# A GEGLU MLP on one core: the 4x2x4 algorithm in the down phase from pass 3 instead of 4, with the preparation of w_down moved to earlier passes

## The chip, the cores and the metric

One core of a Trainium2 chip. The time is device time of one execution in microseconds (us). Most executions of one kernel agree within 0.3%.

Engines by the names of the profile: PE is TensorE (matmul), PEld its weight loads, DVE is VectorE, ACT is ScalarE, POOL is GpSimd, SP is SyncE, which here only issues DMAs. "L827" is line 827 of the kernel's file. Lines shift a little from kernel to kernel, because each edit adds some: the fast gate/up matmuls are L827 before and L843 after, the older gate/up matmuls L620 and L621, the older down phase L966 and L983, the fast one L1074 and L1091.

## The reference

```python
# x: 8 x 1024 x 1024, w_gate and w_up: 1024 x 4096, w_down: 4096 x 1024, all fp32
gate = x @ w_gate
up = x @ w_up
gate = 0.5 * gate * (1 + np.tanh(np.sqrt(2 / np.pi) * (gate + 0.044715 * gate ** 3)))
h = gate * up
return (h @ w_down).astype(np.float32)
```

## The kernel before

The 8192 rows of x are done in eight passes of 1024. Each pass has a gate/up phase (x times both weights, gelu, product: h) and a down phase (h times w_down). All matmuls are fp16 and all of them use fast matrix multiplication, which trades matmuls for additions:

- The older form is a 2x2x2 scheme with seven products in place of eight.
- The newer, "fast" form is a 4x2x4 scheme with 26 products in place of 32. Its operands are sums of blocks. Those of x and h are made anew in each pass; those of the weights are made once, stored in DRAM, and loaded in every later pass.

Gate/up uses the fast form from pass 3 (`FAST = 3`), down from pass 4 (`DFAST = 4`). Before down can use it, all 24 operands of w_down have to be in DRAM. They are made in eight *units*; unit u covers 1/8 of the rows. A unit loads four raw blocks, makes 19 sums on DVE and six signed copies on ACT, one step at a time, and stores 24 results of 128 KB through a few small buffers:

```python
def wd_unit(u, raw, free):
    ...
    def load():
        for k, c, v in ((0, 0, 0), (1, 0, 1), (1, 1, 5)):
            nc.sync.dma_start(out=blk[:, k, c], in_=wdop[2 * v + nb][:, j : j + 2, :])
        nc.gpsimd.dma_start(out=blk[:, 0, 1], in_=wd_eo[0][:, 2 * u : 2 * u + 2, HH:])
    ...
    def step(i):
        stores()                      # DMAs of what the last step made; then free.append(...)
        n, op, a, b = WD_SUMS[i]
        v = at[n] = free.popleft()    # oldest free buffer: waits until its store has landed
        combine(node(n), op, node(a), node(b))          # one DVE sum, 128 x 512 fp16
        ...
        if i % 3 == 0 and i // 3 < len(plain):
            v = free.popleft()
            nc.scalar.activation(...)                   # a signed copy on ACT
```

The steps are dealt out beside the matmuls, counted in *slots*. A slot is one product: 8 matmuls of 256 columns in the fast gate/up phase (0.873 us, 208 slots a phase), 4 matmuls of 512 columns in the older one (0.864 us, 14 slots for each pair of row blocks, 16 pairs, 224 slots a phase).

```python
DFAST = 4
...
UNITS_DOWN = {2: (0, 1), 3: (4, 5)}     # pass: units beside its down phase
UNITS_UP = {3: (2, 3), 4: (6, 7)}       # pass: units beside its fast gate/up phase
...
def gate_up_fast(p):
    if p in UNITS_UP:
        free = deque(hf["s3"][:, 4096 + j * 512 : 4608 + j * 512] for j in range(8))
        for i, u in enumerate(UNITS_UP[p]):
            load, fs = wd_unit(u, hf["s3"][:, 0:4096], free)
            steps[i * 78] = load
            for k, f in enumerate(fs):
                steps[i * 78 + 20 + 3 * k] = f
    for q in range(NQ):               # 8 groups of 26 slots
        ...
        if q == 5 and p + 1 < NPASS:
            extra.setdefault(3, []).append(lambda: cast_x(p + 1))   # 2 MB, on POOL's DMA queue
        owed = quad(p, q, owed, extra)
```

The older gate/up phase makes its weight operands as it goes. In passes 1 and 2 it also makes and stores the fast operands of w_gate and w_up for later (`make_entry`), so its DVE has more to do there:

```python
# pair(p, i): 14 products; what follows a product is emitted after it
1: copy 0     2: copy 1     ...     11: h21     12: h11     13: add s2 0     14: add s2 1
# and, beside them, in even pairs after products 3, 5, 7, 9, in odd pairs after 11, 12, 13, 14:
#   sum_w: four sums of raw weights for the next pair
# in passes 1 and 2 after products 2, 4, ..., 12:  make_entry
# in odd pairs after product 13: load_raw(p, q + 2), 2 x 1 MB (as written, fp16) of raw weights on POOL's DMA queue
```

## Time and profile before

| | us |
|---|---|
| median (4 runs, 2277.09 to 2282.40) | 2277.86 |
| span of the profiled run | 2274.6 |
| gate/up of pass 1, of pass 2 (older form) | 194.87, 193.51 |
| gate/up of pass 3, of pass 4 (fast form, units beside) | 186.84, 186.49 |
| gate/up of passes 5 to 7 (fast form, no units) | 181.65 |
| down of passes 0 to 3 (older form) | 96.69 |
| down of passes 4 to 7 (fast form) | 90.83 |

The lengths are distances between the starts of neighbouring stages in the chain of work in order of time. The busy times of each stage say how much room the other engines have there. Two rows of that view for gate/up of passes 1 and 2 (stretch, length, then busy us of PE, PEld, DVE, ACT, POOL; granted clock, share of the DMA engines, GB/s):

```profile
310.72:505.59 194.87, 193.97 (x897) 87.59 (x896) 150.83 (x222) 111.93 (x184) 60.60 (x43) 1.00 0.83 213
602.28:795.79 193.51, 193.51 (x898) 87.62 (x896) 144.59 (x222) 112.34 (x184) 65.95 (x45) 1.00 0.94 233
```

PE is busy all the time in pass 2 and all but 0.9 us in pass 1. A full stage without waits is thus 193.51 us. DVE is three quarters full on average.

One habit of this view: a matmul of 512 columns is listed with 379 ns, but they start 215.8 ns apart (96.69 us for 448). Where PE really stops, the listed gap is therefore about 0.16 us shorter than the delay of the next matmul. In pass 1 this fits: its three listed gaps (0.19, 0.36 and 0.35 us) and three times 0.16 make 1.38 us, and the stage is 1.36 us longer than pass 2.

### The profile page before, as it was taken

The page shows a single profiled execution, that of the slowest core. Times are in us where ns is not written, and L with a number is a line of the kernel's source. Part 1 is how long each engine was busy: PE and PEld are TensorE (multiplying, and loading weights), DVE is VectorE, ACT ScalarE, POOL GpSimd, SP SyncE. Part 2 cuts the span into 40 slices and gives each one's busy share as a digit, 9 for nine tenths or more (in the row PEclk, how much of TensorE's full clock was granted, in tenths as well). Part 3 has the DMA queues.
Part 4 walks back from the last instruction along what each step waited for, and adds up shares of the span by engine and source line. Part 5 has one row for each costly group of instructions (what it writes and reads, how often), then busy time and mean ns, then how long its engine had stood idle before and what let it go on. Part 6 is the DMA issues. An engine that isn't in the chain of part 4 may idle for free.

```text
span 2274.6 us, 42143 instructions
## 1 busy us (share of the span) xinstructions
PE 2256.0 (99%) x16255; PEld 1589.0 (70%) x16255; DVE 1527.3 (67%) x2170; ACT 963.3 (42%) x1876; POOL 687.4 (30%) x826
## 2 busy tenths in 40 slices
PE   9999999999999999999999999999999999999999
PEld 4444444444444445888458888888888888888888
DVE  5576368782587755776558767766776667866674
ACT  4443135551355522665226651255403553045620
POOL 1342013320133300554005550145402543034520
PEclk9999999999999999999999999999999999999999
DMA  9998959988799999998999999989989899998876
GB/s 231 179 209 206 262 143 221 224 246 263 176 215 225 267 311 350 333 325 318 279 343 333 328 349 305 333 276 288 334 315 323 283 310 314 321 317 274 283 290 230
DMA packets 305306, 632.98 MB, mean 278 GB/s; under 512 B 78992, under 2 KB 181392, under 8 KB 285840
## 3 DMA queue, kind: packets, MB, share of 16 engines
q1 hardware_dynamic: 250048, 556.88, 72.0%
q0 software_dynamic: 55056, 73.41, 19.3%
q8 instruction: 127, 2.08, 0.4%
q14 instruction: 75, 0.61, 0.1%
HBM read 565.18 MB, written 138.41 MB: 309 GB/s over the span
## 4 chain that ended last, share of the span: by engine, by line
PE 95%; DVE 3%; DMA 2%; issue 1%; ACT 0%; SPq 0%; DVEq 0%; ACTq 0%
PE ps L827 39%; PE ps L620 22%; PE ps L966 17%; PE ps L1074 16%; DMA wd_quads<-h_s 1%; DVE ring L349 1%; PE ps L1173 1%; DVE tmp L639 0%; DMA h_a<-in_x_dram 0%; DVE h_a L657 0%; DVE h_s L277 0%; DVE x_sums L277 0%; DVE tmp L789 0%; DVE h_s L410 0%; DVE h_s L414 0%
## 5 line engine op out<-in xcount | busy, mean ns | idle before, releaser
L827 PEld LDWEIGHTS <-ring 128*128 128x128 f16 x8320 | 815.5, 98 | 103.2 <-issue 7.1
L804 POOL TENSOR_TENSOR h_a<-tmp 128x256 f16<-128x256 f32 x640 | 471.9, 756 | 794.7 <-ACT tmp L792 781.0
L827 PE MATMUL ps<-x_sums,ring 128*128 128x256 f16 x5760 | 659.0, 273 | 6.8 <-DVE tmp L789 6.8
L789 DVE TENSOR_TENSOR tmp<-tmp,ps 128x512 f32<-128x512 f32 x640 | 415.2, 683 | 148.8 <-PE ps L827 104.0
L620 PEld LDWEIGHTS <-ring 128*128 128x128 f16 x2632 | 257.3, 98 | 314.5 <-issue 4.6
L774 ACT COPY tmp<-ps 128x512 f32<-128x512 f32 x520 | 304.4, 585 | 220.8 <-PE ps L827 149.9
L620 PE MATMUL ps<-x_sums,ring 128*128 128x512 f16 x1504 | 341.1, 379 | 2.6 <-DVE ring L349 1.7
L792 ACT ACTIVATE tmp<-tmp 128x256 f32<-128x256 f32 x640 | 263.7, 418 | 184.5 <-DVE tmp L789 90.9
L827 PE MATMUL ps<-x_b,ring 128*128 128x256 f16 x2560 | 305.6, 273 | 0.0
L966 PE MATMUL ps<-ring,h_a 128*128 128x512 f16 x1408 | 305.5, 379 | 0.0
L966 PEld LDWEIGHTS <-h_a 128*128 128x128 f16 x1536 | 150.2, 98 | 181.1
L646 POOL TENSOR_TENSOR h_a<-tmp 128x512 f16<-128x512 f32 x94 | 148.9, 1584 | 377.0 <-ACT tmp L644 287.9
L620 PE MATMUL ps<-x_b,ring 128*128 128x512 f16 x1128 | 259.1, 379 | 0.0
L787 DVE TENSOR_TENSOR tmp<-ps,tmp 128x512 f32<-128x512 f32 x240 | 165.4, 689 | 139.0 <-ACT tmp L774 97.8
L639 DVE TENSOR_TENSOR tmp<-ps,tmp 128x512 f32<-128x512 f32 x188 | 127.1, 683 | 136.2 <-ACT tmp L631 133.4
L1074 PEld LDWEIGHTS <-h_a 128*128 128x128 f16 x1792 | 175.3, 98 | 20.3
L1074 PE MATMUL ps<-ring,h_a 128*128 128x256 f16 x1536 | 172.9, 273 | 0.0
L1131 ACT ACTIVATE tmp<-ps 128x512 f32<-128x512 f32 x48 | 28.2, 597 | 290.1 <-PE ps L1074 219.7
L631 ACT COPY tmp<-ps 128x512 f32<-128x512 f32 x188 | 110.1, 586 | 91.5 <-PE ps L620 88.9
L349 DVE TENSOR_TENSOR ring<-ring 128x1024 f16<-128x1024 f16 x188 | 132.8, 721 | 6.0 <-PE ps L966 3.8
L893 ACT ACTIVATE tmp<-ps 128x512 f32<-128x512 f32 x64 | 37.9, 596 | 222.9 <-PE ps L966 222.9
L644 ACT ACTIVATE tmp<-tmp 128x512 f32<-128x512 f32 x94 | 58.8, 626 | 147.5 <-DVE tmp L639 147.4
(94 smaller groups left out, 1557.4 us busy)
## 6 DMA issues: line engine op xcount, KB each, us to landing
ring<-w_ops SPq DMA_DIRECT2D x480, 512.0 KB, 5.0
ring<-wd_quads SPq DMA_DIRECT2D x88, 1024.0 KB, 6.6
ring<-wd_ops SPq DMA_DIRECT2D x49, 1024.0 KB, 7.3
out_dram<-tmp SPq DMA_DIRECT2D x128, 256.0 KB, 6.1
w_ops<-x_sums SPq DMA_DIRECT2D x110, 256.0 KB, 6.3
ring<-in_w_gate_dram POOLq DMA_DIRECT2D x23, 1024.0 KB, 9.0
ring<-in_w_up_dram POOLq DMA_DIRECT2D x23, 1024.0 KB, 17.6
w_ops<-h_s SPq DMA_DIRECT2D x82, 256.0 KB, 5.4
```

Source lines behind the costliest of these rows:

```text
L349: nc.vector.tensor_tensor(o, a, b, op)
L620: nc.tensor.matmul(ps(b, w), lhs[:, k], rhs[:, k, :], start=(first and k == 0), stop=(k == KH - 1), skip_group_check=True,)
L639: nc.vector.tensor_tensor(o, ps("b", w), o, ADD)
L646: nc.gpsimd.tensor_tensor(hq[TO[n]][:, i, :], tmp[:, t[n, 1]], tmp[:, t[n, 0]], MUL)
L774: nc.scalar.copy(tmp[:, t[o[1]]], ps_all[:, bank[o[2]]])
L787: nc.vector.tensor_tensor(d, b, a, SUB)
L789: nc.vector.tensor_tensor(d, a, b, ADD if o[4] == "add" else SUB)
L792: nc.scalar.activation(d, d, GELU, scale=GSC)
L804: nc.gpsimd.tensor_tensor(h, tmp[:, t[o[1]], MQ : 2 * MQ], g, MUL)
L827: nc.tensor.matmul(ps_all[:, bank[c], w * MQ : (w + 1) * MQ], lhs[:, w, k], rhs[:, k], start=(first and w == 0 and k == 0), stop=(k == KH ...
L966: nc.tensor.matmul(ps_all[:, bank[b, g]], lhs[:, j, g * P : (g + 1) * P], dc[:, n, :], start=(first and j == 0), stop=(j == NP - 1), skip_ ...
L1074: nc.tensor.matmul(ps_all[:, bank[c], m * MQ : (m + 1) * MQ], lhs[:, j, m * P : (m + 1) * P], rhs[:, j, :], start=(first and j == 0 and m ...
```

## The change

Its intent: one more down phase in the fast form. For that all units must be ready one pass sooner, so they are dealt out over passes 1 to 3, and their steps get more slots, one more buffer and a cast of x at another time.

```diff
-    DFAST = 4
+    DFAST = 3
+    spare = const.tile([P, 512], FP16, name="spare")
 ...
-        xc[:, j * 1024 : (j + 1) * 1024] for j in range(8, len(X_SUMS))
+        xc[:, j * 1024 : (j + 1) * 1024] for j in range(8, 12)
 ...
+    UNITS_ONE = {1: ((0, 4, 4), (1, 108, 4)), 2: ((3, 20, 6),)}   # pass: (unit, load slot, slots a step)
     def gate_up_one(p):
+        unit_steps = {}
+        if p in UNITS_ONE:
+            free = deque(xc[:, j * 512 : (j + 1) * 512] for j in range(32, 38))
+            free.append(spare)
+            for u, s0, ds in UNITS_ONE[p]:
+                load, fs = wd_unit(u, xc[:, 12288:16384], free)
+                unit_steps[s0] = load
+                for k, f in enumerate(fs):
+                    unit_steps[s0 + 20 + ds * k] = f
 ...
             free = deque(hf["s3"][:, 4096 + j * 512 : 4608 + j * 512] for j in range(8))
+            free.append(spare)
-                steps[i * 78] = load
+                steps[i * 92] = load
-                    steps[i * 78 + 20 + 3 * k] = f
+                    steps[i * 92 + (24 if i else 12) + (3 if i else 4) * k] = f
-            if q == 5 and p + 1 < NPASS:
-                extra.setdefault(3, []).append(lambda: cast_x(p + 1))
+            if q == 3 and p + 1 < NPASS:
+                extra.setdefault(12, []).append(lambda: cast_x(p + 1))
 ...
-    UNITS_DOWN = {2: (0, 1), 3: (4, 5)}
-    UNITS_UP = {3: (2, 3), 4: (6, 7)}
+    UNITS_DOWN = {1: (2,), 2: (4, 5)}
+    UNITS_UP = {3: (6, 7)}
```

(A row of `UNITS_ONE` is unit, slot of its load, slots a step; the first step comes 20 slots after the load. So unit 0 is loaded at slot 4 and has a step at every fourth slot from slot 24 on.)

More of the change, by code (lines that the diff above doesn't have):

```diff
@@ L717, in gate_up_one @@
                 at(8, cast_x, p + 1)
+            for k in range(14):
+                if 14 * i + k in unit_steps:
+                    at(k + 1, unit_steps[14 * i + k])
             if i == NP - 2:
@@ L951, in down @@
                     steps.setdefault(9 + (17 if i else 0) + 5 * k // 6, []).append(f)
-        x_from = 4 if p in UNITS_DOWN else 5 if p < FAST - 1 else 3
+        x_from = 5 if p < FAST - 1 else 4 if p in UNITS_DOWN else 3
         for v, name in enumerate(DSEQ):
```

## The prediction

> **What bounds the kernel now.** I read the page's chain of work first, then the same chain in order of time, then busy time by stage, then the two places where the chain leaves TensorE.
>
> The page says that TensorE is the bound almost everywhere:
> ```profile
> PE 2256.0 (99%) x16255; PEld 1589.0 (70%) x16255; DVE 1527.3 (67%) x2170; ACT 963.3 (42%) x1876; POOL 687.4 (30%) x826
> PE 95%; DVE 3%; DMA 2%; issue 1%; ACT 0%; SPq 0%; DVEq 0%; ACTq 0%
> ```
> So a shorter matmul stream shortens the run one for one. The chain in order of time (start, us, what) gives each stage's length:
> ```profile
> 795.79 96.69 PE ps L966 x448
> 892.48 117.04 PE ps L827 x1072
> ...
> 1013.45 14.23 DMA wd_quads<-h_s
> ...
> 1028.84 50.48 PE ps L827 x448
> 1079.32 96.69 PE ps L966 x448
> ...
> 1296.97 13.76 DMA wd_quads<-h_s
> ...
> 1362.50 90.83 PE ps L1074 x832
> 1453.32 181.65 PE ps L827 x1664
> ```
> L966 is the old down phase (passes 0 to 3), L1074 the 4x2x4 one (4 to 7), L827 the fast gate/up phase (3 to 7). The reader should see three stage lengths that never vary when nothing waits: 96.69, 90.83 and 181.65 us. Gate/up of pass 3 runs from 892.48 to 1079.32, 186.84 us, and that of pass 4 from 1176.01 to 1362.50, 186.49 us: 5.19 and 4.84 us over the clean 181.65. Both have a store of w_down operands in the chain.
>
> What happens there, first on POOL and DVE, then on PE (start, us, operation, [idle before, what ended it]):
> ```profile
> 1008.63 0.59 POOL L249 DMA_DIRECT2D x_half<-in_x_dram  x1
> ```
> ```profile
> 1024.94 0.43 DVE L277 TENSOR_TENSOR h_s<-h_s 128x512 f16<-128x512 f16 x1 [3.49 <-DMA wd_quads<-h_s]
> ```
> ```profile
> 1028.84 3.31 PE L827 MATMUL ps<-x_sums,ring 128*128 128x256 f16 x16 [3.62 <-DVE tmp L789]
> ```
> ```profile
> 1028.50:1032.00 3.50, 3.16 (x17) 2.27 (x17) 3.11 (x6) 1.72 (x4) 1.85 (x3) 0.53 1.05 401
> ```
> The 2 MB cast of the next x starts at 1008.63. Stores issued just before it landed after at most 6.3 us; the three issued from 1009.1 to 1015.2 took 14.1 to 15.8. A unit of w_down has eight small buffers, and at three product slots a step the tightest are taken again 12 slots (12 x 0.873 = 10.5 us) after their store. So DVE waits, evictions behind it come late, PE idles 3.62 us, and the last row shows the granted clock (first number after the engines) at 0.53 right after.
>
> **What the Trainium skill says.**
> - "TensorE: Matmul & The Clock Gate", Back-to-back issue gap: N/2.4 + 2.5 ns when warm. The trace agrees with that isolated form: 96.69/448 = 215.8 ns at 512 columns, 90.83/832 = 109.2 ns at 256.
> - Same page, What's actually happening: an idle window of about 3.4 us puts the array at half rate, a busy one brings it back. The trace agrees: 3.6 us idle, then 0.53. So 3.62 lost idle + half of about 3.4 us = 5.3, against 5.19 measured over the clean stage.
> - "DMA: Bandwidth & Descriptors", Issuing engines are not separate DMA queues: transfers of all issuers share the same 16 engines. The 5-to-14 us jump of stores beside the cast agrees.
>
> **The change part by part.**
> 1. Down of pass 3 uses the 832-matmul form instead of the 448-matmul form: 90.83 - 96.69 = -5.86 us. The extra DVE sums of h lie beside it, as in passes 4 to 7 (DVE busy 72.4 of 90.8 us, no PE wait).
> 2. Eight units have to be ready one pass sooner. Pass 4 makes none now: -4.84 us.
> 3. Pass 3 makes one unit at 4 slots a step (slots 12 to 88) and one at 3 (116 to 173), with nine buffers; the cast moves from slot 133 to slot 90, between them. Counted through the free list, the tightest reuse on DVE becomes 20 and 15 slots (13.1 us), no longer beside the cast. Against stores of 5 to 6 us that is enough: -5.19 us. The second unit's load queues behind the cast (16 us, landing near slot 109) and is needed at slot 116.
> 4. Units 0 and 1 go beside gate/up of pass 1 (a step every 4 slots of 0.864 us), unit 3 beside pass 2 (every 6), unit 2 into down of pass 1, where DVE is busy only 38%. Each step is one DVE sum of 128x512 f16: 0.42 us, 0.34 start to start. Total work is unchanged, but it now meets the sums that make gate/up operands, which saturate DVE in every second pair of row blocks:
> ```profile
> 359.10:371.20 12.10, 12.10 (x58) 5.48 (x57) 12.10 (x19) 6.50 (x11) 5.27 (x4) 1.00 0.89 174
> 371.20:383.30 12.10, 12.10 (x58) 5.50 (x57) 6.85 (x12) 7.55 (x12) 3.40 (x2) 1.00 0.94 262
> ```
> (third busy figure: DVE 12.10 of 12.10, then 6.85.) Here the slack must be counted. At the end of an odd pair DVE runs product, sum, product, sum, operand, then the addition at 359.99; ACT then does a gelu and at 361.23 the copy of the first bank that the next pair's fourth product overwrites:
> ```profile
> 360.70 0.63 ACT L644 ACTIVATE tmp<-tmp 128x512 f32<-128x512 f32 x1 [2.95 <-DVE tmp L639]
> 361.23 1.06 ACT L636 COPY ps<-ps 128x512 f32<-128x512 f32 x2
> ```
> The first copy ends near 361.8; that product starts at 361.86. Slack zero: each step put between h at the eleventh product and that addition costs PE 0.34 us. The instruction order of the changed kernel has one such step in six odd pairs of pass 1 (6 x 0.34 = 2.0 us) and two in pass 2 (0.7). From even to odd pair the copy is ready about 0.61 us early in pass 1 (gelu at 372.21, product at 373.95) and 0.86 in pass 2; three steps cost 1.02, so 0.41 over in five pairs of pass 1 (2.1) and 0.16 in one of pass 2. Two even pairs of pass 1 already show 0.36 us of PE idle and no slack, worth up to 1.2 more; I take half. Pass 1: +4.7. Pass 2: +0.8.
>
> Sum: 2278.2 - 5.86 - 4.84 - 5.19 + 4.7 + 0.8 = 2267.8 us.
>
> **The rivals.**
> - The steps in passes 1 and 2 are absorbed and cost nothing: 2262.3. For it: DVE is busy only 150.8 of 194.9 us in pass 1. Against: the zero slack above.
> - Raw weights become the wait in pass 1. They are loaded when DVE has read the last ones (issues at 360.70 and 361.63, the slower landing after 19.0 us, at 380.6) and are needed one double pair after 357.54, at 381.7: margin 1.1 us. The unit's stores add about 0.8 MB in that stretch. If they delay the load 2 us, six double pairs lose some 1.4 us each instead of 0.8: about 2271.5. Against: the loads and stores share the engines, but for the first 6 us of a load hardly any store is in flight, and later the store side already has a backlog, so a longer one need not slow the load.
> - The pass-3 stall does not go but moves, say to the second unit's load behind the cast: +5.2, about 2273. Against: 7 slots (6 us) of margin.
> - Stores in pass 1 land too late for seven buffers reused after 12 slots (10.4 us); the slowest operand store there took 9.4 by my reading of landings, so this is close. If DVE waits there and PE idles past a window, each place costs 3 to 5 us: up to 2278.
>
> **Range and chances.** The three savings (15.9 us together) are read off stages that repeat to 0.01 us, so I trust them; the uncertainty is what passes 1 and 2 give back, 0 to 12 us. Range 2262 to 2275, middle 2267.8, a ratio of 0.995. A 2% change would be 45 us; nothing here is that large either way. Faster by over 2%: 0.01; within 2%: 0.98; slower: 0.01.
>
> **What would show it.** Steps 1 to 3: the chain in time shows down of pass 3 at 90.83, and gate/up of passes 3 and 4 at 181.65 in one piece without stores of w_down operands, with no clock dip between the start and the end. Step 4: gate/up of pass 1 goes from 194.87 to about 199.6 us with small PE waits on ACT's copy of a bank, pass 2 from 193.51 to about 194.3. I am wrong if passes 1 and 2 stay as they are (slack misread), if PE waits there on the raw weights or on stores, or if a piece of pass 3 still waits for a DMA.

## The result, and the profile after

| | before | after | predicted |
|---|---|---|---|
| median of four runs, us | 2277.86 | 2272.30 | 2267.8 (2262 to 2275) |
| lowest to highest | 2277.09 to 2282.40 | 2270.24 to 2274.07 | |
| ratio of fast runs (95% interval) | | 0.9971 (0.9954 to 0.9988) | 0.995 |
| gate/up of pass 1 | 194.87 | 205.17 | about 199.6 |
| gate/up of pass 2 | 193.51 | 195.58 | about 194.3 |
| gate/up of pass 3 | 186.84 | 181.69 | 181.65 |
| down of pass 3 | 96.69 | 90.83 | 90.83 |
| gate/up of pass 4 | 186.49 | 181.65 | 181.65 |

The profiled runs are not the medians: the kernel before was profiled in an execution of 2276.39 us, below all of its four timed ones, the changed kernel in one of 2273.83 us, above its own median. So the stages below add up to a gain of only some 3 us (the two spans differ by 2.6 us), where the medians differ by 5.6. The ratio is the mean time of one kernel's fast runs over that of the other's of the same rounds, so it is not quite the ratio of the medians.

Passes 3 and 4 first. In the chain of work in order of time (start, us, what) of the changed kernel they are three unbroken pieces:

```profile
905.41 181.68 PE ps L843 x1664
1087.10 90.83 PE ps L1091 x832
1177.92 181.65 PE ps L843 x1664
```

The stores of w_down operands have left the chain there and down of pass 3 has the length of the fast form. Together that is 5.15 + 5.86 + 4.84 = 15.85 us gained. The same kind of rows as above, for gate/up of passes 1 and 2 of the changed kernel, show what was paid for it:

```profile
311.28:516.45 205.17, 197.09 (x897) 87.83 (x896) 162.00 (x260) 117.46 (x196) 71.26 (x45) 0.99 0.94 243
...
613.14:808.72 195.58, 194.44 (x898) 87.58 (x896) 156.86 (x241) 114.45 (x190) 65.19 (x46) 1.00 1.00 252
```

Pass 1 is 10.30 us longer than before and pass 2 2.07 us. DVE has only 11 and 12 us more work; PE has lost 8.08 us to gaps in pass 1, and the clock column reads 0.99. What PE waited for in these two passes (us in total, times, longest):

```profile
PE ps L621 <- DVE tmp L640: 7.0, 8, 2.8
PE ps L621 <- ACT ps L637: 1.8, 5, 0.5
```

L637 is the copy of a bank on ACT that the prediction named; L640 is an addition on DVE. But the longest wait, 2.8 us, is far above 0.34 us a step. Two rows of DVE with their idle time, and the PE rows that follow from them (start, us, engine, line, operation, [idle before, what ended it]):

```profile
381.96 0.42 DVE L278 TENSOR_TENSOR x_sums<-x_sums 128x512 f16<-128x512 f16 x1 [4.11 <-DMA wd_quads<-x_sums]
...
437.55 0.69 DVE L350 TENSOR_TENSOR ring<-ring 128x1024 f16<-128x1024 f16 x1 [2.77 <-DMA ring<-in_w_up_dram]
```
```profile
390.12 1.02 PE L621 MATMUL ps<-x_sums,ring 128*128 128x512 f16 x4 [1.28 <-DVE tmp L640]
```
```profile
442.18 4.12 PE L621 MATMUL ps<-x_sums,ring 128*128 128x512 f16 x11 [2.78 <-DVE tmp L640]
```

At 381.96 a step of unit 0 waited for a buffer whose store had not landed; DVE fell behind by as much, and PE stopped for 1.28 us at 390.12. At 437.55 DVE waited for raw weights of w_up, and PE stopped for 2.78 us. The chain in order of time has that load in it, with its landing time:

```profile
414.55 22.91 DMA ring<-in_w_up_dram
```

In the kernel before, the slowest load of this kind in pass 1 took 19.0 us. Finally the clock: the stretch after the longest gap, of the same view as above.

```profile
442.00:446.00 4.00, 3.82 (x11) 1.41 (x11) 4.00 (x9) 2.06 (x5) 3.99 (x2) 0.57 0.96 140
```

The granted clock is 0.57 in these 4 us. The clock records have one stretch of 3.4 us at half rate from 442.0 on, which costs half of that, 1.7 us. Of the changed kernel's four runs two have a mean clock of 1.000 (2270.24 and 2270.76 us) and two 0.999 (2273.83, the profiled one, and 2274.07), so this dip comes in some executions and not in others. The groups are 3.4 us apart, though, so at 1.7 us the dip can be only half of the difference; the rest was not looked into. The kernel of experiment 1 has the same pass 1 and was profiled without a dip: 203.35 us instead of 205.17, with the same kinds of gaps (1.47, 1.70 and 1.24 us are the longest). Single profiles of this pass thus differ by about 2 us.

So the cost that the prediction forecast and two of its rivals seem to have come true at once in pass 1: direct cost of steps, late buffers, late raw weights. The experiments separate them.

### The profile page after: what moved, and what is told of

The parts are those of the page before. It is cut to its first block, busy times and chain, and to the rows that moved or that the text cites. A ratio compares the mean times of both kernels' runs of the same rounds, so it can differ in the third digit from the quotient of the medians.

```text
span 2272.0 us, 42804 instructions
## 1 busy us (share of the span) xinstructions
PE 2251.1 (99%) x16639; PEld 1625.5 (72%) x16639; DVE 1560.5 (69%) x2188; ACT 956.3 (42%) x1868; POOL 693.0 (31%) x826
## 3 DMA queue, kind: packets, MB, share of 16 engines
q0 software_dynamic: 55056, 73.41, 19.4%
## 4 chain that ended last, share of the span: by engine, by line
PE 90%; DVE 5%; DMA 3%; issue 1%; ACT 1%; SPq 0%; POOL 0%; DVEq 0%; POOLq 0%; ACTq 0%
PE ps L843 40%; PE ps L1091 20%; PE ps L621 16%; PE ps L983 13%; DMA ring<-in_w_up_dram 2%; DVE ring L350 2%; DVE tmp L640 1%; DVE h_s L278 1%; DMA wd_quads<-x_sums 1%; PE ps L1190 1%; DVE h_a L658 1%; DVE x_sums L278 1%; DMA h_a<-in_x_dram 0%; DMA w_ops<-h_s 0%; ACT ps L637 0%
## 5 line engine op out<-in xcount | busy, mean ns | idle before, releaser
L621 PEld LDWEIGHTS <-ring 128*128 128x128 f16 x2632 | 257.5, 98 | 326.6 <-issue 18.4
L647 POOL TENSOR_TENSOR h_a<-tmp 128x512 f16<-128x512 f32 x94 | 158.5, 1686 | 362.8 <-ACT tmp L645 223.9
L1091 PEld LDWEIGHTS <-h_a 128*128 128x128 f16 x2240 | 219.1, 98 | 25.4
L983 PE MATMUL ps<-ring,h_a 128*128 128x512 f16 x1024 | 222.3, 379 | 0.0
L1091 PE MATMUL ps<-ring,h_a 128*128 128x256 f16 x1920 | 216.1, 273 | 0.0
L983 PEld LDWEIGHTS <-h_a 128*128 128x128 f16 x1152 | 112.7, 98 | 135.9
L640 DVE TENSOR_TENSOR tmp<-ps,tmp 128x512 f32<-128x512 f32 x188 | 127.7, 684 | 114.2 <-ACT tmp L632 111.4
L1148 ACT ACTIVATE tmp<-ps 128x512 f32<-128x512 f32 x60 | 35.4, 597 | 362.5 <-PE ps L1091 274.4
L1160 DVE SCALAR_TENSOR_TENSOR tmp<-ps,tmp 128x512 f32<-128x512 f32 x120 | 81.1, 690 | 97.5 <-PE ps L1091 66.7
L1091 PE MATMUL ps<-ring,x_sums 128*128 128x256 f16 x1120 | 126.4, 273 | 0.0
```

The costliest lines, as they stand in the source:

```text
L621: nc.tensor.matmul(ps(b, w), lhs[:, k], rhs[:, k, :], start=(first and k == 0), stop=(k == KH - 1), skip_group_check=True,)
L640: nc.vector.tensor_tensor(o, ps("b", w), o, ADD)
L647: nc.gpsimd.tensor_tensor(hq[TO[n]][:, i, :], tmp[:, t[n, 1]], tmp[:, t[n, 0]], MUL)
L983: nc.tensor.matmul(ps_all[:, bank[b, g]], lhs[:, j, g * P : (g + 1) * P], dc[:, n, :], start=(first and j == 0), stop=(j == NP - 1), skip_ ...
L1091: nc.tensor.matmul(ps_all[:, bank[c], m * MQ : (m + 1) * MQ], lhs[:, j, m * P : (m + 1) * P], rhs[:, j, :], start=(first and j == 0 and m ...
```

## The experiments

Every kernel was run on the chip with a profile. Where a kernel gives the right result it was also timed in alternation with the kernel before. Single runs, and wrong results, are said to be so; of those only stage lengths are used, and their untouched stages (181.7 to 182.0 and 90.8 us) show that they were not disturbed.

### 1. The old down form in pass 3, all else changed

```diff
-    DFAST = 3
+    DFAST = 4
```

> The changed kernel with down of pass 3 in the old form again; everything else of the change stays. My theory (savings and losses add up by stage): down of pass 3 takes 96.69 us instead of 90.83, the rest as in the changed kernel, so 2272.3 + 5.9 = 2278 us, the time of the kernel before. Rival (the new down form also has costs of its own at its borders): less than 5.9 us between the two.

Measured: 2278.03 us, ratio 1.0003 (0.9988 to 1.0018). Down of pass 3 is 96.69 us again. As expected: the term of the algorithm is 5.86 us and has no cost at its borders, and without it the rest of the change is worth nothing that these runs can tell from zero (the interval is some 3 us to either side). The 5.86 us itself is read from the stage; the two totals come from different calls. Gate/up of passes 3 and 4 gained about 10 us and passes 1 and 2 gave about as much back.

### 2. The cast of x alone, in the kernel before

```diff
-            if q == 5 and p + 1 < NPASS:
-                extra.setdefault(3, []).append(lambda: cast_x(p + 1))
+            if q == 3 and p + 1 < NPASS:
+                extra.setdefault(12, []).append(lambda: cast_x(p + 1))
```

> The kernel before with one thing moved: the cast of the next x at slot 90 instead of 133 of each fast gate/up phase. Theory (the cast slows the stores of the second unit, nothing else): gate/up of passes 3 and 4 takes 181.7 us each instead of 186.8 and 186.5, in all 2278 - 10 = 2268 us, faster than the whole change. Rival (8 buffers at 3 slots a step are too few in any case, more slots are the cure): a store wait of some us stays in passes 3 and 4, 2272 us or more.

Measured: 2266.40 us (2266.17 to 2267.84), ratio 0.9955 (0.9940 to 0.9969). This two-line edit of the kernel before has a lower time than the whole change. The intervals of the two ratios overlap a little (0.9940 to 0.9969, 0.9954 to 0.9988); the stages tell them apart: 9.95 us gained in passes 3 and 4 here, 15.85 gained less 12.37 given back in the changed kernel. Its chain in order of time has both phases in one piece:

```profile
892.57 181.73 PE ps L827 x1664
1074.30 96.69 PE ps L966 x448
1170.99 181.65 PE ps L827 x1664
```

Eight buffers, three slots a step and a second unit at slot 78 are enough, then, for PE, as long as the 2 MB cast isn't under way when the buffers come round. (DVE still waits 1.5 us in all for stores; PE never stops.)

### 3. The complement: new slots and ninth buffer, the cast where it was

```diff
+            free.append(spare)
-                steps[i * 78] = load
+                steps[i * 92] = load
-                    steps[i * 78 + 20 + 3 * k] = f
+                    steps[i * 92 + (24 if i else 12) + (3 if i else 4) * k] = f
```

(on the kernel before, in passes 3 and 4)

> The kernel before with the other half of the change to its fast gate/up phases: units at slots 12 (four slots a step) and 116 (three) and a ninth buffer, in passes 3 and 4, while the cast of x stays at slot 133. It is the complement of the run that moved the cast alone. Theory (the cast, at slots 133 to 151, is what makes stores take 14 to 16 us; 13.1 us of reuse on DVE and 10.5 on ACT is still under that): DVE waits of 1 to 3 us on stores stay in both passes, PE idles 0 to 2 us in each, gate/up 181.7 to 184 us instead of 186.8 and 186.5, in all 2270 to 2274 us. Rival (slots and buffer are a full cure): no store wait, 181.7 each, 2266 us as with the cast moved.

Measured: 2272.56 us (2272.03 to 2274.69), ratio 0.9989 (0.9973 to 1.0004); gate/up of pass 3 183.4 us, of pass 4 185.8. Waits in these two passes, on DVE and on PE:

```profile
DVE h_s L278 <- DMA wd_quads<-h_s: 4.5, 3, 2.6
```
```profile
PE ps L828 <- DVE tmp L790: 4.8, 5, 1.5
```

The stores still take up to 16.6 us beside the cast, longer than the 13.1 us of reuse, and DVE still waits, though less (4.5 us in the two passes, 8.9 before); the signed copies on ACT wait for stores as well, 4.8 us. So the cast is the cause, and more slots are a weaker cure than another time for the cast: about 4 of the 10 us here (3.4 in pass 3, 0.7 in pass 4), 10 in the run above. Pass 4 lost more than I expected (185.8 against at most 184).

### 4. Unit 1's load away from the raw load

```diff
-                unit_steps[s0] = load
+                unit_steps[97 if u == 1 else s0] = load
```

> The changed kernel with the load of unit 1 in pass 1 at slot 97 instead of slot 108, which is two slots before a load of raw weights. Theory (that raw load landed after 22.9 us because it queues behind the unit's load): the PE gap of 2.8 us at 442 and the clock dip after it go, gate/up of pass 1 takes 200 to 201 us instead of 205.2, in all 2268 to 2269. Rival (the unit's stores slow every raw load): the raw load at 414 still takes over 21 us, and pass 1 stays at 204 to 205.

Measured: 2269.68 us (2269.23 to 2272.99), ratio 0.9971 (0.9956 to 0.9986). Gate/up of pass 1 is 200.19 us, the gap of 2.8 us is down to 0.2, the clock is 1.00, and the raw load took 19.8 us instead of 22.9. It looked like a clean confirmation that the raw load queues behind the unit's load. Experiments 7 and 8 show that this reading was too simple.

### 5. Sums without stores, and stores without sums

Both give a wrong result, one run each. In the first, units beside gate/up of passes 1 and 2 load and add but store nothing:

```diff
             for v, n in made:
-                nc.sync.dma_start(out=wdq[...], in_=v...)
+                if keep:                # False for the units of passes 1 and 2
+                    nc.sync.dma_start(out=wdq[...], in_=v...)
```

> Wrong result on purpose: the changed kernel, in which the units beside gate/up of passes 1 and 2 make their sums but store nothing (their places in DRAM are filled from other data in down of pass 1, so only gate/up of passes 1 and 2 is to be read). Theory (steps on the tight DVE stretch cost PE 0.34 us each, by themselves): gate/up of pass 1 takes 194.9 + 4.7 = about 199.6 us, with small gaps at each pair's fourth product, no store wait and no late raw load. Rival (the transfers are the whole cost): 195 to 196 us.

Measured: gate/up of pass 1 202.64 us. The store wait is gone, but the late raw load is not: 22.8 us, with a gap of 2.78 us and a dip of the clock. My expectation was wrong in that, since I had left the unit's *loads* in. Without gap and dip (2.78 + 0.16 + 1.7 us) the phase would be 198.0.

In the second, units load and store but add nothing (the buffers hold zeros):

```diff
-            combine(node(n), op, node(a), node(b))
+            if sums:                    # False for the units of passes 1 and 2
+                combine(node(n), op, node(a), node(b))
```

> Wrong result on purpose: the changed kernel, in which the units beside gate/up of passes 1 and 2 load and store as before but make no sums (buffers hold zeros). Theory (late raw loads from the unit's load and its stores): the raw load issued two slots after the unit's load still lands after over 21 us, and gate/up of pass 1 takes 196 to 199 us. Rival (sums are the whole cost): 194.9 us.

Measured: gate/up of pass 1 199.64 us, with three PE gaps (0.24, 2.44, 1.08 us), each after a DVE wait on raw weights of w_up, and one dip of 1.7 us. The raw loads took 20.0, 20.4, 19.4, 22.9, 18.9 and 21.3 us; in the kernel before they took 18.8, 19.0, 18.2, 18.4, 17.2 and 17.2. So transfers alone make the raw weights late, and DVE work costs PE as well, by subtraction: 198.0 less 194.87. Neither rival is the whole.

### 6. More buffers in pass 1

```diff
             free.append(spare)
+            if p == 1:                  # two of the twelve fp32 tiles lent: four more buffers
+                lent = [tmp_free.pop() for _ in range(2)]
+                for v in lent:
+                    h = tmp[:, v].bitcast(FP16)
+                    free.extend(h[:, j * 512 : (j + 1) * 512] for j in range(2))
```

> The changed kernel with eleven buffers instead of seven for the units of pass 1 (four of them in two of the twelve fp32 tiles, lent for that pass). The tightest reuse on DVE goes from 12 slots (10.4 us) to 24. Theory: the DVE wait of 4.1 us on a store at 382 and the PE gap of 1.3 us at 390 go, the rest stays: gate/up of pass 1 203.9 us with a clock dip, 202.2 without, in all some 1.3 us less than the changed kernel. Rival: nothing changes, the wait is taken by the next thing on DVE.

Measured: 2272.03 us (2269.91 to 2273.76), ratio 0.9984 (0.9970 to 0.9997). In the profile the store wait of 4.1 us is gone, the gap of 1.28 us is 0.20, and gate/up of pass 1 is 202.98 us with its clock dip, 2.2 us less than in the changed kernel. The total doesn't show it; the late raw load and the dip, which come and go, can hide what was saved. (A first version had a tile of its own for six buffers and didn't fit into the core's memory.) The row of the phase, for comparison with experiment 8:

```profile
311.19:514.17 202.98, 196.98 (x898) 87.80 (x896) 162.59 (x260) 117.30 (x196) 73.80 (x45) 0.99 0.95 246
```

### 7. Both repairs, and the same kernel again

> The changed kernel with both repairs to pass 1: unit 1's load at slot 97 and eleven buffers. What is left is then the direct cost of the steps, which the prediction put at 4.7 us. Theory (terms add up): no store wait on DVE, no raw load over 21 us, no clock dip, gate/up of pass 1 at 198.5 to 199.6 us against 194.3 to 194.9 in the kernel before, gaps only of 0.2 to 0.5 us at the fourth products, in all 2268 us. Rival (the waits only move): pass 1 stays at 200 or more.

Measured: 2268.09 us (2266.37 to 2271.82), ratio 0.9970 (0.9954 to 0.9985). The total is what I expected, but not for the reason: gate/up of pass 1 is 201.20 us, and the raw load took 22.6 us again, with a gap of 2.78 us, though the unit's load on POOL's queue had landed 2 us before the raw load was issued. The landing row of the two raw loads at that place (w_gate, then w_up; the largest is w_up's):

```profile
DMA to landing us min/median/max: 14.3/18.5/22.6
```

"It queues behind the unit's load" can't be all.

> The kernel with unit 1's load at slot 97 and eleven buffers once more, unchanged: does the landing of the raw load of slot 110 repeat? If it is fixed by the program, 22 to 23 us and a PE gap of 2.8 us again; if it varies from run to run, some value between 19 and 23 and another gap, and no cause may be read from a single profile of it.

Measured (one run): 21.7 us, a gap of 1.84 us, gate/up of pass 1 202.38 us. The landing varies by about a microsecond from run to run, but the load is late both times.

### 8. No load for unit 1 at all

A wrong result, one run, with eleven buffers:

```diff
-                unit_steps[s0] = load
+                if u != 1:
+                    unit_steps[s0] = load
```

> Wrong result on purpose: the changed kernel with eleven buffers in pass 1, and no load for unit 1 (its steps work on what unit 0 left there). It asks whether the raw load of slot 110, which took 22.6 to 23.0 us in four runs and 19.8 in one, is late because of that unit's load. If yes: it lands after 18.5 to 19.5 us like the others, the DVE wait on it and the PE gap of 2.8 us are gone, gate/up of pass 1 takes 198 to 199 us. If no (the steps' stores and the shifted time of the load do it): still over 22 us and a gap of over 2 us.

Measured: the raw load took 17.6 us, no DVE wait on it is left, and gate/up of pass 1 is 198.72 us. The landing row for the two raw loads at that place, and the phase, both of this kernel:

```profile
DMA to landing us min/median/max: 10.0/13.8/17.6
```
```profile
311.21:509.93 198.72, 195.65 (x897) 87.54 (x896) 160.97 (x260) 117.39 (x196) 66.88 (x44) 1.00 0.95 246
```

The four transfers of unit 1's load are thus the cause of the late raw load, issued just before it (slot 108) or thirteen slots earlier (slot 97): the earlier slot didn't take them out of the way in experiment 7. This rests on one run without the load, but its 17.6 us lie below all eight profiles with it (19.8 to 23.0 us). The stores of the same unit are not needed for the lateness: in experiment 5 nothing of the units was stored in pass 1, and with the load at slot 108 this raw load still took 22.8 us. The profiles show one trace of the way. These are the first 3 us of the two raw loads in experiment 7 (first run) and here, the last two figures being the share of the DMA engines and GB/s:

```profile
411.17:414.17 3.00, 3.00 (x16) 1.36 (x14) 3.00 (x4) 2.19 (x4) 2.99 (x3) 1.00 1.06 349
411.94:414.94 3.00, 3.00 (x16) 1.36 (x14) 3.00 (x4) 2.17 (x4) 2.99 (x3) 1.00 0.65 136
```

With the unit's load at slot 97 the engines are still full of earlier transfers, at 349 GB/s, when the raw load begins; without it they are not. Three of the load's four transfers are issued on SP's queue, ahead of stores; I read this as the backlog that they leave. But experiment 4 has the same full start (1.03, 355 GB/s) and a raw load of 19.8 us, so it isn't the whole. Why the same move gave 19.8 us there stays open; DVE and PE were also 1.5 us later, because of the store wait, so less of the late landing was felt.

### 9. Steps only where DVE is idle

```diff
-    UNITS_ONE = {1: ((0, 4, 4), (1, 108, 4)), 2: ((3, 20, 6),)}
+    UNITS_ONE = {1: 0, 2: 3}
+    QUIET = [14 * i + d for i in range(1, 14, 2) for d in (2, 5, 8)]
 ...
-                    unit_steps[s0 + 20 + ds * k] = f
+                unit_steps[QUIET[k]] = f
-    UNITS_DOWN = {1: (2,), 2: (4, 5)}
+    UNITS_DOWN = {1: (1, 2), 2: (4, 5)}
```

> The changed kernel with the early units placed elsewhere: unit 1 goes from gate/up of pass 1 to down of pass 1 (two units there, as in pass 2), and units 0 and 3 have their steps only at the third, sixth and ninth product of the odd pairs, where DVE is idle, three steps per 24 us. Theory (steps on the DVE stretch from the eleventh product of an odd pair through the even pair cost PE, as do raw loads made late by them): gate/up of pass 1 is back at 195 us, of pass 2 at 193.5, down of pass 1 stays at 96.7, in all 2262.3 us. Rival (their transfers alone slow the raw loads): pass 1 stays above 198, 2266 or more.

Measured: 2271.26 us (2269.69 to 2273.85), ratio 0.9978 (0.9962 to 0.9995). Gate/up of pass 1, down of pass 1 and gate/up of pass 2, by busy time:

```profile
311.04:505.63 194.59, 193.81 (x897) 87.58 (x896) 156.67 (x241) 114.49 (x190) 62.97 (x44) 1.00 0.90 235
505.63:607.99 102.36, 98.40 (x449) 44.09 (x448) 52.34 (x81) 17.87 (x32) 6.68 (x7) 0.98 1.03 291
607.99:804.59 196.60, 194.14 (x898) 87.57 (x896) 152.40 (x241) 114.77 (x190) 67.96 (x46) 1.00 1.00 254
```

The theory held for gate/up of pass 1: a whole unit beside it (DVE 156.7 us instead of 150.8) costs nothing. But my repair put new waits elsewhere. A second unit in down of pass 1 waits for its stores there, which come late: SP's queue issues four transposing loads of the next x from 546.62 us on, for 13.06 us, and no store in that time. PE stops for 3.3 us and the clock dips. And in pass 2 I had put unit 3's load at slot 0, behind three loads of raw weights; it took 18.9 us, its first step made DVE wait, and PE stopped for 1.95 us.

### 10. A version without those two faults

```diff
+    QUIET3 = [14 * i + d for i in range(1, 14, 2) for d in (2, 5, 8)]
+    QUIET8 = [14 * i + d for i in (3, 5, 7, 9, 11, 13) for d in range(1, 9)]
+    UNITS_ONE = {
+        1: ((0, 0, QUIET3[:20]),),
+        2: ((1, 20, QUIET8[:20]), (3, 103, QUIET8[24:44])),
+    }
```

(and eleven buffers as in experiment 6, in both passes; down of pass 1 keeps its one unit)

> The changed kernel with unit 0 alone beside pass 1 (third, sixth and ninth product of odd pairs), units 1 and 3 beside gate/up of pass 2 (second to ninth product of odd pairs 3 to 13, eleven buffers), and down of pass 1 with one unit as in the changed kernel. The margin of raw loads in pass 2 was 4.7 us against 1.1 in pass 1. Theory: gate/up of pass 1 194.8 us, down of pass 1 96.7, gate/up of pass 2 193.5 to 195, in all 2262 to 2264 us, faster than the changed kernel and than the kernel before with its cast moved (2266.4). Rival (two units in one pass cost some 2 us or more wherever they are): pass 2 over 196, 2265 or more.

Measured: 2264.05 us (2263.78 to 2265.12), ratio 0.9950 (0.9937 to 0.9964). The same three stages:

```profile
311.18:505.77 194.59, 193.82 (x897) 87.52 (x896) 156.75 (x241) 114.48 (x190) 62.97 (x44) 1.00 0.90 235
505.77:602.47 96.70, 96.70 (x450) 43.83 (x448) 44.86 (x62) 14.76 (x26) 5.97 (x6) 1.00 0.98 271
602.47:798.42 195.95, 194.15 (x897) 87.63 (x896) 164.96 (x260) 118.05 (x196) 66.74 (x47) 1.00 1.07 272
```

Nothing is paid in pass 1, 2.4 us in pass 2. That is more than I expected there (193.5 to 195) and just under the rival's 196; two PE gaps of 0.62 and 1.08 us after an addition on DVE make most of it. The total is at the upper end of my range. This kernel has the lowest median of all here and is clearly faster than the kernel before. Its ratio overlaps a little with the changed kernel's; the stages tell them apart. In them it keeps 13.4 of the 15.85 us. The medians of its call are 11.3 us apart; the rest of the difference was not looked into. Against experiment 2 (2266.40, with its own runs of the kernel before) it is not shown to be faster: the ratios 0.9950 and 0.9955 have overlapping intervals.

## Why the prediction was right or wrong

**The range** held: 2272.30 us, inside 2262 to 2275, and within 2%. The middle was 4.5 us too low, by the medians. In the stages of the profiled run the miss is larger: passes 1 and 2 give back 12.37 us where 5.5 were forecast, which is also just outside the 0 to 12 us that I had allowed. That the total still lies well inside the range owes something to the width of the range and to the faster executions without the dip.

**Steps 1 to 3, the savings**, were right to 0.04 us: 90.83, 181.69 and 181.65 us, as read off stages of the kernel before that had no units. Experiment 1 shows the first term by itself. Experiments 2 and 3 show the mechanism that the prediction gave for the other two: cast, slow stores, buffers that come round too soon, DVE, PE, clock. What they add is the shares. The prediction told the new slots, the ninth buffer and the moved cast in one breath; the cast alone brings all of the gain, the slots alone less than half. The small sum for pass 3 (3.62 + 1.7 = 5.3 against 5.19) fits a little too easily: 3.62 is a listed gap and 0.16 too short, and in the 3.5 us from 1028.80 on the clock was 0.58, which costs 1.5 and not 1.7; together 5.25.

**Step 4, what passes 1 and 2 give back**, is the term that was mis-sized: +4.7 and +0.8 us predicted, +10.30 and +2.07 measured. The direct cost that it stood for was right (3.9 us of the 10.30 in pass 1, where 4.7 were forecast); what it left at zero, waits for buffers and for raw weights, is the larger part. Taken apart run by run, gate/up of pass 1:

| | us | difference |
|---|---|---|
| changed kernel | 205.17 | |
| with eleven buffers (experiment 6) | 202.98 | 2.2: buffers reused before their store has landed |
| and without unit 1's load (experiment 8) | 198.72 | 4.3: late raw weights, of which 1.7 a clock dip |
| kernel before | 194.87 | 3.9: the steps themselves, and their stores |

Each line is one profile, and the same pass 1 has differed by 2 us between two of them, so the shares are good to a microsecond or two.

The last line is what I had worked out as 4.7 from the slack, and the slack itself was read well: in experiment 8 four of the six gaps at the fourth products after an odd pair are 0.19 or 0.20 us as listed (the others 0.52 and 0.33), so 0.35 with the 0.16 us that the listing leaves out, against 0.34 worked out; those after an even pair are mostly 0.18 to 0.27, so 0.34 to 0.43, against 0.41. The half of 1.2 us that I had added for two pairs did not come.

One pair of transitions shows the direct cost in the changed kernel, DVE rows from an odd pair's eleventh product on:

```profile
464.09 0.83 DVE L350 TENSOR_TENSOR ring<-ring 128x1024 f16<-128x1024 f16 x1
464.84 0.41 DVE L278 TENSOR_TENSOR x_sums<-x_sums 128x512 f16<-128x512 f16 x1
465.18 0.68 DVE L658 TENSOR_TENSOR h_a<-ps,tmp 128x512 f16<-128x512 f32 x1
```

The second row is the step: it starts 0.34 us before the next, which is what it pushes everything after it back by.

**The rivals.** "Absorbed" fell: in experiment 8 DVE waits for no raw load (the slowest took 20.6 us) and the steps still cost 3.9 us, and experiment 5 less its gap and dip has 3.1. But it is true of steps that lie where DVE is idle (experiments 9 and 10). "Raw weights become the wait" came true, for one of six loads at 2.8 us and one at 1.1, not for each at 1.4; I had looked to the units' stores and not to the transfers of a unit's own load, which experiment 8 shows to be what matters for the longer wait. The wait of 1.1 us, on the sixth raw load, points to the stores: that load took 17.4 us in the run without them (experiment 5) and 19.4 to 21.6 us in the eight with the same steps and stores. "Stores land too late for seven buffers" came true once (the store was issued at 371.73 us and took 10.1 us; DVE came to the step that needs its buffer some 6 us after that issue and stood for 4.11 us, until 381.96), and it cost 1.28 us of PE and not 3 to 5. The prediction had counted 12 slots, 10.4 us, from that store to the reuse. But slots are counted in PE's products, and DVE doesn't keep to them: it had fallen behind in the full pair and caught up in the next, so that it went from the sum of the step that issued the store (371.97 us) to the step that needed the buffer (377.85) in 5.9 us, three steps later. "The stall in pass 3 moves" did not happen. I had weighed these against each other; they came together.

**The clock.** I gave it to passes 3 and 4 before, and did not think of it coming back in pass 1. It cost 1.7 us in the profiled run, and it goes with the slower of the two groups of the changed kernel's runs, of whose distance (3.4 us) it explains half.

In pass 2 the mis-sizing (2.07 against 0.8 us) was not taken apart further: with transfers only it took 194.06 us, so by that one run most of it belongs to the sums.

## What to carry to other kernels

When work is moved beside a stage that looks roomy by its mean busy time, count the slack at the point where the bound engine meets the work (here DVE to ACT to PE at one product in fourteen) and put the work where the helper engine is idle: unit 0 cost 3.7 us in the changed kernel and nothing in experiments 9 and 10. (Before unit 1 is loaded and with unit 0 all but done, the 20 matmuls that end the seventh pair start 85.92 us into the phase, at 397.20; in the kernel before 82.23, at 392.95. In experiments 9 and 10 the whole phase takes 0.28 us less than before.) Transfers moved with it count as well, the loads as much as the stores, against the margin of whatever already arrives just in time. And before a large rearrangement, try its smallest part alone: here two lines that moved one DMA gained 9.95 us in their stages, and the whole change, in its profiled run, 15.85 less 12.37 (ratios 0.9955 and 0.9971, with intervals that overlap a little).

## What the Trainium skill lacked or had wrong

- "TensorE: Matmul & The Clock Gate", section Back-to-back issue gap: it gives about 131 ns a matmul as the sustained rate of a stream of weight loads and matmuls at N = 512, and says that the isolated formula, about 216 ns, over-counts there. The runs show 215.8 ns (96.69 us for 448) sustained through every down phase of the older form with one weight load a matmul; the isolated formula is the right one here.
- Same page, section "Why this matters for your kernels": it asks for no PE gap over about 3 us. The runs show a dip to half rate after listed gaps of 2.78 us (changed kernel), 2.44 (experiment 5) and 1.84 (experiment 7, second run), and none after 2.78 us in the first run of experiment 7, the same kernel. A gap below 3 us was thus not safe here, and the same gap passed once and cost 1.7 us another time.
- "DMA: Bandwidth & Descriptors": that all issuers share 16 engines is told, but not how long a small store then waits. Here 128 KB stores landed after 4.4 to 6.3 us just before a 2 MB casting DMA of POOL's queue and after 14.1 to 15.8 us just behind its start (up to 16.6 in experiment 3).
- No page says that a gap on PE, as a profile lists it, is shorter than the delay of the next matmul, here by about 0.16 us (512-column matmuls are listed with 379 ns and start 215.8 ns apart).
